# A decoder trunk on one core: the MLP's second product with two of its seven products on shared PSUM banks, and the LayerNorm ahead of the MLP on ScalarE

## The chip, the cores and the metric

The kernel runs on one core of a Trainium2 chip. TensorE (PE) multiplies into PSUM, VectorE (DVE), ScalarE (ACT) and GpSimd (POOL) work element by element, SyncE (SP) issues DMAs. Each engine runs its own instructions in their order and waits for others by semaphores. The metric is the time of one execution on the device in microseconds; the median of several runs is compared.

## The reference

Two layers of a post-norm decoder: a token mixer, then an MLP, with a LayerNorm behind each. The sequence has 1024 rows, the model 1024 columns, the MLP 4096. Cut to what the change touches:

```python
def layer_norm(x, g, b):
    mu = jnp.mean(x, axis=-1, keepdims=True)
    var = jnp.mean(jnp.square(x - mu), axis=-1, keepdims=True)
    return (x - mu) * lax.rsqrt(var + LN_EPS) * g + b

for l in range(DEPTH):
    ...
    h = layer_norm(DEEPNORM_ALPHA * h + mix, ln1_g[l], ln1_b[l])
    ff = jnp.square(jax.nn.relu(h @ w_up[l])) @ w_down[l]
    h = layer_norm(DEEPNORM_ALPHA * h + ff, ln2_g[l], ln2_b[l])
```

All is float32. The kernel splits each operand into a high and a low part and makes three matmuls (high·high, high·low, low·high) for one product.

## The kernel before

**Data.** The residual stream is `zs`, eight tiles `z` of 128 rows by 1024 columns. Eight PSUM banks of 128x512 come from four rings: `pg` has three (allocated by `p_g`), `ps` two, `pt` two, `po` one.

**The MLP by chunks.** `w_up`'s 4096 columns are done in eight chunks of 512 (`NCH`). For a chunk, `up_steps(c)` makes the hidden values of all rows and `down_steps(c)` multiplies them by the 512 rows of `w_down` and adds the outcome to `zs`. Both treat their matrices as 2x2 quarters and make seven products of quarters in place of eight (the scheme of Strassen and Winograd), whose results are added to the quarters of the output. The first chunk's up product is plain (`up_plain(0)`, in two halves of the rows, 96 matmuls to a half and a column block of 512) and the last chunk's down product is plain too (`last_down`), so a layer has seven calls of `down_steps`: one behind `up_plain`, and six that alternate with `up_steps`. `run` goes through the steps; for each it first prepares the next step's operands and then does the matmuls.

**A down product.** The seven steps stand at the end of `down_steps`, in the order first, second, p5, p6, p3, p7, p4. `prep` copies the left operand `a` to its high part on ACT (L1161, `sa`), subtracts on DVE for the low part, and splits the weights into `wdh` (ACT) and `wdl` (DVE). Where a step's operand is a sum (the tiles `s` and `u`, the weights `wd`), DVE forms it just ahead of that. A step makes four groups, one for each 128 of its 512 rows, 6 matmuls each, so 24 a step and 168 in all. `bank` tells where a group accumulates: "x" is a set of four banks (two `ps`, two `pt`) which p6, p7 and p4 add to after the first step; "f" is a fresh `pg` for each group. After each group, DVE adds the bank to the z quarters named in the step's tail, (th, d): rows 4·th to 4·th+3 of the tiles, half d of the columns (`add(zc, zc, ps)`, L971 in the profile). A bank can be filled anew, or added to, once that read is done.

**The LayerNorm ahead of the MLP.** Behind the output projection, for each pair of z tiles, `ln_unit` takes the statistics (`ln_stats`) and normalizes in place on DVE (L154). `to_act` transposes the tiles on PE by blocks of 128x128 into `pt`, applies gain and offset on ACT on the way out (`f`, L212), and splits the outcome into `mh` (ACT, L215) and `ml` (DVE, L216), the MLP's operands. Behind `up_plain(0)` in the code, `residual` multiplies each normalized z by the row `gb` and adds `bb` on DVE (L817, L818); `sums_of_input` forms sums of the `f` tiles for later chunks.

**What sets the order.** The instructions of each engine are put in order by a scheduler ahead of time, with its own estimate of when each can run and with priorities (`boost()` around weight splits). The order in the code only breaks ties, so the order on each engine can change far from an edit.

Of the kernel before, what the change touches and what calls it, by code (L numbers as in the profile page):

```python
# [9 lines left out]
F32 = mybir.dt.float32  # L10
# [5 lines left out]
ALU = mybir.AluOpType  # L16
# [28 lines left out]
def trunk_kernel(ctx, tc, x, ln_in_g, ln_in_b, w_in, conv_w, conv_b, rg_wa, rg_ba, rg_wx, rg_bx, rg_lambda,  # L45
# [26 lines left out]
    def t_z(shape, nm, dt=F32):  # L72
        return big.tile(shape, dt, tag="z", name=nm, bufs=NZ)

    def t_u(dt, shape, nm):
        return big.tile(shape, dt, tag="u", name=nm, bufs=4)
# [4 lines left out]
    def t_s(shape, nm):  # L81
        return sm.tile(shape, F32, tag="s", name=nm, bufs=10)

    def p_g():
        return pg.tile([P, 512], F32, tag="g", name="pg")
# [19 lines left out]

    K = {}
    K["eps"] = cpool.tile([P, 1], F32, name="eps")
    V.memset(K["eps"], LN_EPS)
    A.activation(t_s([P, 1], "warm"), K["eps"], AF.Sqrt)

# [17 lines left out]
            V.scalar_tensor_tensor(out=r, in0=t, scalar=1.5, in1=r, op0=ALU.add, op1=ALU.mult)  # L128
        return r

    def ln_stats(zs):

        n = len(zs)
        st, mv = t_s([P, n, 2, 6], "lnst"), t_s([P, n, 2], "lnmv")
        for i, z in enumerate(zs):
            for j in range(2):
                V.bn_stats(out=st[:, i, j, :], in_=z[:, 512 * j:512 * j + 512])  # L137
            V.bn_aggr(out=mv[:, i, :], in_=st[:, i].rearrange("p a b -> p (a b)"))

        var = mv[:, :, 1]  # L140
        ve, r, t = t_s([P, n], "lnve"), t_s([P, n], "lnr"), t_s([P, n], "lnt")
        A.activation(r, var, AF.Sqrt, bias=K["eps"])
        V.tensor_scalar(out=ve, in0=var, scalar1=LN_EPS, scalar2=-0.5, op0=ALU.add, op1=ALU.mult)
        V.reciprocal(out=r, in_=r)
        V.tensor_tensor(out=t, in0=r, in1=r, op=ALU.mult)  # L145
        V.tensor_tensor(out=t, in0=t, in1=ve, op=ALU.mult)  # L146
        V.scalar_tensor_tensor(out=r, in0=t, scalar=1.5, in1=r, op0=ALU.add, op1=ALU.mult)  # L147
        return mv[:, :, 0], r
# [728 lines left out]
    for l in range(DEPTH):  # L877
# [43 lines left out]
        gb, bb = residual_rows(ln1_g[l], ln1_b[l])  # L921
        act = Act("m")

        keep = [[t_u(F32, [P, 4, 512], f"f{h}{g}") for g in range(2)] for h in range(2)]
        for cqs in ((0, 1), (2,), (3,)):
            ws = [load_cols(w_out[l], [(cq * 256, 256)], "wo") for cq in cqs]
            for nt in range(NT):
                for i, cq in enumerate(cqs):
                    ps = p_g()[:, :256]
                    gemm_tm(ps, ws[i], ya, nt)  # L930
                    zc = zs[nt][:, cq * 256:cq * 256 + 256]
                    V.tensor_tensor(out=zc, in0=zc, in1=ps, op=ALU.add)
                if cqs[-1] == 3 and nt % 2:
                    ln_unit(zs[nt - 1:nt + 1])
                    to_act(act, zs[nt - 1:nt + 1], nt - 1, *[c[:, 8 * l:8 * l + 8] for c in ln1], keep)

        nxt = Act("x") if l + 1 < DEPTH else None
        NCH = DFF // 512
# [203 lines left out]
        def down_steps(c, base):  # L1142

            def t_v(nm):
                return t_wf(nm) if c == 0 else t_z([P, 2, 512], nm)

            b, op, s_ = {}, {}, []
            x = []

            def load(j, k):  # L1150
                t = t_raw(f"wd{j}{k}").rearrange("p (f d) -> p f d", f=2) if j == 0 else t_v(f"wd{j}{k}")
                r0 = c * 512 + 256 * j
                nc.sync.dma_start(out=t, in_=w_down[l][r0:r0 + 256, 512 * k:512 * k + 512].rearrange("(f p) d -> p f d", p=P))
                b[j, k] = t

            def prep(a, w):
                av = []
                for f in range(2):
                    hi, lo = [mid.tile([P, 512], F32R, tag="m", name=f"sa{p}", bufs=NM) for p in range(2)]
                    src = a.parts[f] if isinstance(a, Quarter) else a[:, f]  # L1160
                    A.activation(hi, src, AF.Copy)  # L1161
                    sub(lo, src, hi.bitcast(F32))
                    av.append((hi, lo))
                hi, lo = split_w(w.rearrange("p f d -> p (f d)"), "wd")
                op["a"], op["w"] = av, [v.rearrange("p (f d) -> p f d", f=2) for v in (hi, lo)]

            def step(pre, operands, bank, first, *sums):
                got = []

                def p_():  # L1170
                    pre()
                    prep(*operands())
                    got.append((op["a"], op["w"]))

                def r_():
                    a, w = got[0]
                    if not x:
                        x.extend((p_s(), p_s(), p_t(), p_t()))
                    for i in range(4):
                        t = slice(i * P, i * P + P)  # L1180
                        ps = x[i] if bank == "x" else p_g()
                        mm3_on(ps, [((a[f][0][:, t], a[f][1][:, t]), (w[0][:, f, :], w[1][:, f, :])) for f in range(2)], first)
                        for th, d in sums:
                            zc = zs[4 * th + i][:, 512 * d:512 * d + 512]
                            add(zc, zc, ps)
                return p_, r_

            def loads():
                for jk in ((0, 0), (1, 0), (0, 1), (1, 1)):
                    load(*jk)  # L1190

            def p5():
                s_.append(t_v("s1"))
                base[1][0].by(lambda u, v, s: add(s, u, v), base[1][1], s_[0])
                sub(b[0, 0], b[0, 1], b[0, 0])

            def p6():
                base[0][0].by(lambda u, s: sub(s, s, u), s_[0])
                sub(b[0, 0], b[1, 1], b[0, 0])

            def p3():
                base[0][1].by(lambda u, s: sub(u, u, s), s_[0])

            def p7():
                base[1][0].by(lambda u, v: sub(u, v, u), base[0][0])
                sub(b[0, 1], b[1, 1], b[0, 1])

            def p4():
                sub(b[1, 0], b[1, 0], b[0, 0])

            nop = lambda: None
            return [
                step(loads, lambda: (base[0][0], b[0, 0]), "x", True, (0, 0)),
                step(nop, lambda: (base[0][1], b[1, 0]), "f", True, (0, 0)),
                step(p5, lambda: (s_[0], b[0, 0]), "f", True, (1, 1), (0, 1)),
                step(p6, lambda: (s_[0], b[0, 0]), "x", False, (0, 1)),
                step(p3, lambda: (base[0][1], b[1, 1]), "f", True, (0, 1)),
                step(p7, lambda: (base[1][0], b[0, 1]), "x", False, (1, 1)),
                step(p4, lambda: (base[1][1], b[1, 0]), "x", False, (1, 0))]

# [35 lines left out]
                        nc.sync.dma_start(out=spill[nt - 1 + i], in_=zp[i])  # L1256

        base = up_plain(0)
        for z in zs:
            residual(z, gb, bb)  # L1260
        sums_of_input()
        moving = [None]
        fixed = [fetch(1, t_u), fetch(2, t_u)]
# [87 lines left out]
```

## Time and profile before

| | |
|---|---|
| median of 3 runs | 2537.6 us (2537.27 to 2538.57) |
| the profiled execution | 2534.94 us, span of its instructions 2533.2 us |
| PE busy | 2409.7 us (95%), 14692 matmuls |
| DVE busy | 1803.8 us (71%) |
| ACT busy | 1105.7 us (44%) |
| POOL busy | 122.1 us (5%) |

A timeline row gives the start of an instruction (or of several alike in a row, x2), its length, its engine, its line and its operands as output <- inputs; in brackets, how long its engine sat idle before it and what it waited for. Matmuls overlap: the length of one is its own time from entry to end, and the distance of two starts is what it costs in a row. The same holds for the other engines, where the next instruction may start before the last has drained. A window row gives the length of a stretch and each engine's busy time in it with the count of starts, then the clock that was granted to TensorE (1.00 is 2.4 GHz, .50 is 1.2 GHz).

### The profile page before, as it was taken

The numbers are of one execution on the slowest core, as the hardware profiler recorded it, in microseconds if no ns is written. First come the engines' busy times: TensorE is split into PE (matmuls) and PEld (weight loads), VectorE is DVE, ScalarE is ACT, GpSimd is POOL, SyncE is SP. The second block draws the span as 40 slices with busy tenths as digits, with TensorE's granted clock in tenths as the row PEclk, the third lists the DMA queues.
The fourth block names the chain that finished last, engine by engine and source line by source line (L and its number), as shares of the span: only waits on it lengthen the run. The fifth ranks groups of instructions, "written<-read, shape, count | busy, mean of one in ns | idle before, by whom it ended". The sixth has DMA issues, their size and how long they took to land. (4 is left out here: it accounts for less than half of the span.)

```text
span 2533.2 us, 36546 instructions
## 1 busy us (share of the span) xinstructions
PE 2409.7 (95%) x14692; PEld 2014.7 (80%) x14692; DVE 1803.8 (71%) x3105; ACT 1105.7 (44%) x1710; POOL 122.1 (5%) x190
## 2 busy tenths in 40 slices
PE   7999999999899999999999999999998999999997
PEld 6887888897678777877798877889976777777875
DVE  6578764747976787778745868456577867787768
ACT  6433556415444334433462346472353444344442
POOL 0002000000100000000000110000001000000003
PEclk9999999999999999999999989999999999999999
DMA  5215102211833223232221321121226333223222
GB/s 190 64 50 169 35 28 84 68 51 34 282 108 125 92 75 133 100 115 78 92 81 34 113 97 39 40 84 51 67 98 223 112 114 120 92 75 133 100 83 83
DMA packets 131073, 241.41 MB, mean 95 GB/s; under 512 B 8924, under 2 KB 89432, under 8 KB 122712
## 3 DMA queue, kind: packets, MB, share of 16 engines
q1 hardware_dynamic: 110128, 135.55, 16.6%
q0 software_dynamic: 19648, 102.80, 11.4%
q8 instruction: 116, 1.90, 0.3%
q10 hardware_dynamic: 1128, 0.72, 0.1%
q14 instruction: 53, 0.43, 0.1%
HBM read 201.29 MB, written 37.75 MB: 94 GB/s over the span
## 5 line engine op out<-in xcount | busy, mean ns | idle before, releaser
L261 PE MATMUL pg<-wdh,sa 128*128 128x512 f32 x672 | 233.9, 409 | 31.4 <-DVE z L971 24.7
L222 ACT ACTIVATE wuh<-wu 128x1024 fp32r<-128x1024 f32 x106 | 112.2, 1059 | 319.4 <-DVE wu L968 187.9
L223 DVE TENSOR_TENSOR wul<-wu,wuh 128x1024 fp32r<-128x1024 f32 x106 | 130.3, 1229 | 147.0 <-ACT wuh L222 67.9
L261 PEld LDWEIGHTS pg<-wdh,sa 128*128 128x128 f32 x672 | 128.7, 192 | 84.1 <-DVE z L971 31.3
L222 ACT ACTIVATE wdh<-wd 128x1024 fp32r<-128x1024 f32 x120 | 126.6, 1056 | 132.8 <-DVE wd L968 59.5
L223 DVE TENSOR_TENSOR wdl<-wd,wdh 128x1024 fp32r<-128x1024 f32 x120 | 147.5, 1229 | 44.9 <-PE pt L261 22.4
L261 PE MATMUL ps<-wdh,sa 128*128 128x512 f32 x448 | 149.4, 398 | 26.7 <-DVE z L971 21.0
L252 PE MATMUL pg<-woh,yh 128*128 128x256 f32 x512 | 147.7, 290 | 1.0 <-DVE bvg L637 1.0
L971 DVE TENSOR_TENSOR z<-z,pg 128x512 f32<-128x512 f32 x224 | 146.9, 696 | 0.0
L253 PE MATMUL pg<-wol,yh 128*128 128x256 f32 x512 | 146.3, 287 | 0.0
L261 PE MATMUL pt<-wdh,sa 128*128 128x512 f32 x448 | 145.8, 391 | 0.0
L254 PE MATMUL pg<-woh,yl 128*128 128x256 f32 x512 | 145.5, 287 | 0.0
L261 PE MATMUL pg<-s,wuh 128*128 128x512 f32 x448 | 137.7, 389 | 1.4 <-ACT wuh L222 1.4
L261 PE MATMUL pt<-s,wuh 128*128 128x512 f32 x448 | 137.9, 389 | 0.0
L261 PE MATMUL pg<-wdl,sa 128*128 128x512 f32 x336 | 132.3, 401 | 0.0
L261 PEld LDWEIGHTS ps<-wdh,sa 128*128 128x128 f32 x448 | 82.9, 188 | 54.6 <-issue 26.5
L968 DVE TENSOR_TENSOR sa<-u,sa 128x512 fp32r<-128x512 f32 x140 | 91.5, 698 | 29.5 <-ACT sa L1161 29.5
L261 PE MATMUL pg<-mh,wuh 128*128 128x512 f32 x280 | 109.2, 390 | 0.0
L261 PE MATMUL pg<-ml,wuh 128*128 128x512 f32 x280 | 109.1, 390 | 0.0
L261 PE MATMUL pg<-mh,wul 128*128 128x512 f32 x280 | 108.6, 389 | 0.0
L252 PEld LDWEIGHTS pg<-woh,yh 128*128 128x128 f32 x512 | 99.1, 194 | 1.9 <-PE pt L715 1.4
L253 PEld LDWEIGHTS pg<-wol,yh 128*128 128x128 f32 x512 | 99.3, 194 | 0.1
(388 smaller groups left out, 6833.0 us busy)
## 6 DMA issues: line engine op xcount, KB each, us to landing
s<-sd POOLq DMA_DIRECT2D x64, 1024.0 KB, 6.9
wu<-in_w_up_dram SPq DMA_DIRECT2D x64, 512.0 KB, 3.8
wd<-in_w_down_dram SPq DMA_DIRECT2D x64, 512.0 KB, 3.6
sd<-sx POOLq DMA_DIRECT2D x32, 512.0 KB, 3.8
spill<-z SPq DMA_DIRECT2D x16, 512.0 KB, 4.7
wb<-in_w_in_dram SPq DMA_DIRECT2D x16, 512.0 KB, 6.3
rs<-spill POOLq DMA_DIRECT2D x32, 256.0 KB, 4.2
resid<-rs POOLq DMA_DIRECT2D x32, 256.0 KB, 3.6
```

The lines of the kernel that those rows point to most:

```text
L222: A.activation(hi, raw, AF.Copy)
L223: V.tensor_tensor(out=lo, in0=raw, in1=hi.bitcast(F32), op=ALU.subtract)
L252: T.matmul(ps, ah, bh, start=(i == 0), stop=False)
L253: T.matmul(ps, ah, bl, start=False, stop=False)
L254: T.matmul(ps, al, bh, start=False, stop=(i == n - 1))
L261: T.matmul(ps, a, b, start=(first and i == 0 and j == 0), stop=(i == n - 1 and j == 2), skip_group_check=not first)
L968: V.tensor_tensor(out=out, in0=x, in1=y, op=ALU.subtract)
L971: V.tensor_tensor(out=out, in0=x, in1=y, op=ALU.add)
```

## The change

There are two parts. In `down_steps` the fifth product gets four banks of its own, "y": three `pg` and the `po`. They are added to z's quarter (1,1) only and then kept; p3 goes on accumulating on them (no `start`), and its adds to (0,1) bring both products. So the fifth product's four adds to (0,1) are gone.

In the LayerNorm ahead of the MLP the statistics are kept in constant tiles `mv` and `rs`. ACT writes the normalized rows to new tiles `zu` (scale r, offset −mean·r, formed by a small DVE instruction), which the transposes read; z itself stays as it was. The residual becomes (z − mean)·gb, then times r plus bb, as two DVE instructions a tile, which need z and the statistics and no longer wait for the transposes.

```diff
     K["eps"] = cpool.tile([P, 1], F32, name="eps")
+    K["mv"], K["rs"] = cpool.tile([P, NT, 2], F32, name="mv"), cpool.tile([P, NT], F32, name="rs")
...
-    def ln_stats(zs):
+    def ln_stats(zs, mv=None, r=None):
...
+        mv, rs = K["mv"], K["rs"]
...
                 if cqs[-1] == 3 and nt % 2:
-                    ln_unit(zs[nt - 1:nt + 1])
-                    to_act(act, zs[nt - 1:nt + 1], nt - 1, *[c[:, 8 * l:8 * l + 8] for c in ln1], keep)
+                    pair = slice(nt - 1, nt + 1)
+                    mean, r = ln_stats(zs[pair], mv[:, pair, :], rs[:, pair])
+                    nb = t_s([P, 2], "lnnb")
+                    V.scalar_tensor_tensor(out=nb, in0=mean, scalar=-1.0, in1=r, op0=ALU.mult, op1=ALU.mult)
+                    zu = [t_z([P, DM], "zu") for _ in range(2)]
+                    for i in range(2):
+                        A.activation(zu[i], zs[nt - 1 + i], AF.Identity, scale=r[:, i:i + 1], bias=nb[:, i:i + 1])
+                    to_act(act, zu, nt - 1, *[c[:, 8 * l:8 * l + 8] for c in ln1], keep)
...
-            x = []
+            x, y = [], []
...
                         t = slice(i * P, i * P + P)
-                        ps = x[i] if bank == "x" else p_g()
+                        if bank == "y" and first:
+                            y.append(p_g() if i < 3 else p_o())
+                        ps = x[i] if bank == "x" else y[i] if bank == "y" else p_g()
...
-                step(p5, lambda: (s_[0], b[0, 0]), "f", True, (1, 1), (0, 1)),
+                step(p5, lambda: (s_[0], b[0, 0]), "y", True, (1, 1)),
                 step(p6, lambda: (s_[0], b[0, 0]), "x", False, (0, 1)),
-                step(p3, lambda: (base[0][1], b[1, 1]), "f", True, (0, 1)),
+                step(p3, lambda: (base[0][1], b[1, 1]), "y", False, (0, 1)),
...
         base = up_plain(0)
-        for z in zs:
-            residual(z, gb, bb)
+        for i, z in enumerate(zs):
+            V.scalar_tensor_tensor(out=z, in0=z, scalar=mv[:, i, 0:1], in1=gb, op0=ALU.subtract, op1=ALU.mult)
+            V.scalar_tensor_tensor(out=z, in0=z, scalar=rs[:, i:i + 1], in1=bb, op0=ALU.mult, op1=ALU.add)
```

The order of the engines' instructions moves with it. First DVE in a steady down product, from the adds of the second product on (a number behind a name tells tiles apart, and differs between the two kernels). Before:

```order
L971 TENSOR_TENSOR z<-z,pg 128x512
L968 TENSOR_TENSOR sa_10140<-s_10132,sa_10139 128x512
L971 TENSOR_TENSOR z<-z,pg 128x512
L968 TENSOR_TENSOR wd_10040<-wd_10046,wd_10040 128x1024
L971 TENSOR_TENSOR z<-z,pg 128x512
L968 TENSOR_TENSOR s_10132<-s_10132,u_9864 128x1024
L971 TENSOR_TENSOR z<-z,pg 128x512
L968 TENSOR_TENSOR wd_10042<-wd_10042,wd_10040 128x1024
L971 TENSOR_TENSOR z<-z,pg 128x512 x2
L223 TENSOR_TENSOR wdl<-wd_10040,wdh 128x1024
L968 TENSOR_TENSOR u_9933<-u_9933,s_10132 128x1024
L971 TENSOR_TENSOR z<-z,pg 128x512 x2
```

After:

```order
L981 TENSOR_TENSOR z<-z,pg 128x512
L978 TENSOR_TENSOR sa_9546<-s_9538,sa_9545 128x512
L981 TENSOR_TENSOR z<-z,pg 128x512
L978 TENSOR_TENSOR wd_9446<-wd_9452,wd_9446 128x1024
L981 TENSOR_TENSOR z<-z,pg 128x512
L978 TENSOR_TENSOR s_9538<-s_9538,u_9270 128x1024
L981 TENSOR_TENSOR z<-z,pg 128x512
L981 TENSOR_TENSOR z<-z,po 128x512
L978 TENSOR_TENSOR wd_9448<-wd_9448,wd_9446 128x1024
L981 TENSOR_TENSOR z<-z,pg 128x512
L226 TENSOR_TENSOR wdl<-wd_9446,wdh 128x1024
L978 TENSOR_TENSOR u_9339<-u_9339,s_9538 128x1024
```

Before, pairs of adds of `pg` follow the second product's four single ones, one ahead of `wdl` and the next behind it; now a `po` add and single `pg` adds stand there.

Next PE in the same place, from the end of the fifth product into the sixth (`ps`, `pt`) and the first matmul of the third. Before:

```order
L261 MATMUL ps<-wdh,sa_9617 128x512 x2
L261 MATMUL pt<-wdh,sa_9617 128x512 x2
L261 MATMUL pg<-wdh,sa_9571 128x512
L261 MATMUL pg<-wdl,sa_9571 128x512
L261 MATMUL pg<-wdh,sa_9572 128x512
L261 MATMUL pg<-wdh,sa_9575 128x512
L261 MATMUL pg<-wdl,sa_9575 128x512
L261 MATMUL pg<-wdh,sa_9576 128x512
L261 MATMUL ps<-wdl,sa_9617 128x512 x2
L261 MATMUL pt<-wdl,sa_9617 128x512 x2
L261 MATMUL pg<-wdh,sa_9666 128x512
```

After:

```order
L264 MATMUL pg<-wdh,sa_9546 128x512
L264 MATMUL ps<-wdh,sa_9587 128x512 x2
L264 MATMUL pt<-wdh,sa_9587 128x512 x2
L264 MATMUL ps<-wdl,sa_9587 128x512 x2
L264 MATMUL pt<-wdl,sa_9587 128x512 x2
L264 MATMUL pg<-wdh,sa_9632 128x512 x2
L264 MATMUL po<-wdh,sa_9632 128x512
```

Before, the fifth product's last six matmuls stand between the sixth's first four and next four; now they are ahead of the sixth product, and the third's first matmuls go to `pg` twice and `po` once, at the place where one `pg` matmul stood.

Last, ACT in layer 0 around the end of `up_plain`'s first half, whose last group is read by the u of line 991 (1001 in the changed file). Before:

```order
L212 ACTIVATE f_5230<-pt,lnc_848 128x256
L215 ACTIVATE mh_6200<-f_5230 128x2x256
L212 ACTIVATE f_5230<-pt,lnc_848 128x256
L215 ACTIVATE mh_6200<-f_5230 128x2x256
L991 ACTIVATE u_6351<-pg 128x512
L212 ACTIVATE f_5231<-pt,lnc_848 128x256
L992 ACTIVATE u_6351<-u_6351 128x512
L212 ACTIVATE f_5231<-pt,lnc_848 128x256 x2
L215 ACTIVATE mh_6220<-f_5231 128x2x256
```

After:

```order
L1001 ACTIVATE u_6361<-pg 128x512
L215 ACTIVATE f_5233<-pt,lnc_850 128x256
L944 ACTIVATE zu<-z,lnnb,rs 128x1024
L215 ACTIVATE f_5233<-pt,lnc_850 128x256
L1002 ACTIVATE u_6361<-u_6361 128x512
L218 ACTIVATE mh_6228<-f_5233 128x2x256
L215 ACTIVATE f_5232<-pt,lnc_850 128x256
L218 ACTIVATE mh_6228<-f_5233 128x2x256
L215 ACTIVATE f_5232<-pt,lnc_850 128x256 x2
L218 ACTIVATE mh_6208<-f_5232 128x2x256
```

The last group of the first half is u_6351 before and u_6361 after; the second half's first operand is mh_6200 before and mh_6208 after. Before, the last two parts of that operand stand ahead of u_6351; now they are behind u_6361 (the first of them is the last row here), with a zu of 128x1024 in between.

## Rows read from the trace of the kernel before

**Rows 1.** The page, part 1: busy time, share of the span, instructions
```profile
PE 2409.7 (95%) x14692; PEld 2014.7 (80%) x14692; DVE 1803.8 (71%) x3105; ACT 1105.7 (44%) x1710; POOL 122.1 (5%) x190
```

**Rows 2.** PE's waits over the span: engine, line, releaser: sum, times, longest (us)
```profile
PE pg L261 <- DVE z L971: 24.7, 27, 3.7
PE ps L261 <- DVE z L971: 21.0, 12, 1.8
PE po L506 <- DVE df L497: 8.8, 5, 4.1
```

**Rows 3.** Timeline of PE, a steady chunk: start, us, operation, [idle before <- releaser]
```profile
984.65 0.84 PE L261 MATMUL pg<-wdh,sa 128*128 128x512 f32 x3
...
989.04 0.50 PE L261 MATMUL pg<-wdh,sa 128*128 128x512 f32 x1 [0.16 <-DVE z L971]
...
999.60 0.47 PE L261 MATMUL pg<-wdh,sa 128*128 128x512 f32 x1 [0.99 <-DVE z L971]
1000.11 0.73 PE L261 MATMUL ps<-wdh,sa 128*128 128x512 f32 x2
...
1009.68 0.47 PE L261 MATMUL ps<-wdh,sa 128*128 128x512 f32 x1 [1.79 <-DVE z L971]
...
1016.58 0.39 PE L261 MATMUL pg<-mh,wuh 128*128 128x512 f32 x1
...
1018.85 0.39 PE L261 MATMUL pg<-ml,wuh 128*128 128x512 f32 x1
...
1080.49 0.47 PE L261 MATMUL pg<-wdh,sa 128*128 128x512 f32 x1 [1.01 <-DVE z L971]
```

**Rows 4.** Windows, down product and up product: start:end, length, busy time of each engine
```profile
979.00:1027.00 48.00, 44.95 (x192) 35.35 (x191) 46.22 (x61) 17.33 (x23) 0.00 (x0) 1.00 0.19 63
1027.00:1060.00 33.00, 33.00 (x147) 27.35 (x146) 15.92 (x19) 16.77 (x21) 2.11 (x4) 1.00 0.48 168
```

**Rows 5.** Timeline of DVE in the same chunk
```profile
995.89 1.23 DVE L223 TENSOR_TENSOR wdl<-wd,wdh 128x1024 fp32r<-128x1024 f32 x1
997.03 1.23 DVE L968 TENSOR_TENSOR u<-u,s 128x1024 f32<-128x1024 f32 x1
...
1008.83 1.30 DVE L971 TENSOR_TENSOR z<-z,ps 128x512 f32<-128x512 f32 x2
1010.03 1.30 DVE L971 TENSOR_TENSOR z<-z,pt 128x512 f32<-128x512 f32 x2
```

**Rows 6.** Groups by line and shape, count | busy, mean ns; durations of two lines
```profile
L1161 ACT ACTIVATE sa<-u 128x512 fp32r<-128x512 f32 x140 | 79.8, 621 | 31.9 <-PE pt L261 25.2 <-DVE u L968 4.8 <-DVE sa L968 1.1
...
L212 ACT ACTIVATE f<-pt,lnc 128x256 f32<-128x256 f32 x64 | 34.2, 561 | 32.8 <-PE pt L207 32.4
...
L154 DVE TENSOR_SCALAR z<-z,lnmv,lnr 128x1024 f32<-128x1024 f32 x32 | 25.1, 824 | 0.3
...
L170 ACT ACTIVATE z<-z,lnnb,lnr x7: 1240/1245/1247, 2484.1 to 2521.6; 128x1024 f32<-128x1024 f32 x7
...
L165 DVE SCALAR_TENSOR_TENSOR z<-z,lnr,lnp x2: 747/750/752, 2528.5 to 2529.2; 128x512 f32<-128x512 f32 x2
```

**Rows 7.** Windows at layer 0's LayerNorm ahead of the MLP; then PE's timeline there
```profile
585.00:590.00 5.00, 3.58 (x14) 2.04 (x15) 5.00 (x7) 4.93 (x11) 0.00 (x0) 0.91 0.44 141
590.00:595.00 5.00, 4.05 (x14) 2.14 (x12) 5.00 (x9) 3.94 (x9) 0.00 (x0) 0.50 0.19 68
595.00:600.00 5.00, 4.93 (x14) 4.01 (x15) 5.00 (x9) 2.15 (x6) 0.00 (x0) 0.57 0.00 0
...
595.41 0.78 PE L253 MATMUL pg<-ml,wuh 128*128 128x512 f32 x1
```

**Rows 8.** Window of layer 0's first chunk, down product; then DVE's timeline there
```profile
627.00:690.00 63.00, 53.67 (x212) 40.97 (x211) 62.79 (x78) 29.86 (x41) 11.73 (x22) 0.92 0.81 271
...
627.82 2.36 DVE L817 TENSOR_TENSOR z<-z,lnp 128x1024 f32<-128x1024 f32 x2
...
631.82 2.35 DVE L818 TENSOR_TENSOR z<-z,lnp 128x1024 f32<-128x1024 f32 x2
```

More of the change, by code (lines that the diff above doesn't have):

```diff
@@ L129, in rsqrt_small @@
         return r
-    def ln_stats(zs):
+    def ln_stats(zs, mv=None, r=None):
         n = len(zs)
-        st, mv = t_s([P, n, 2, 6], "lnst"), t_s([P, n, 2], "lnmv")
+        st = t_s([P, n, 2, 6], "lnst")
+        mv = t_s([P, n, 2], "lnmv") if mv is None else mv
         for i, z in enumerate(zs):
@@ L140, in ln_stats @@
         var = mv[:, :, 1]
-        ve, r, t = t_s([P, n], "lnve"), t_s([P, n], "lnr"), t_s([P, n], "lnt")
+        ve, t = t_s([P, n], "lnve"), t_s([P, n], "lnt")
+        r = t_s([P, n], "lnr") if r is None else r
         A.activation(r, var, AF.Sqrt, bias=K["eps"])
```

## Prediction

> **What bounds the kernel now.** I began with the busy times of the engines: TensorE (PE) is busy for 2409.7 of the 2533.2 us span [rows 1]. So PE sets the time, and all that a change with the same matmuls can win lies in PE's idle time and in matmuls that run slower than they could. The table of PE's waits [rows 2] says where that is: the two largest entries, 24.7 and 21.0 us, are MLP matmuls (L261) that wait for VectorE (DVE) to add a finished product to z (L971), since only then is a PSUM bank free.
>
> Next, one steady chunk of the MLP on PE's timeline [rows 3]. A `pg` matmul waits .16 us at 989.04 and .99 at 999.60, a `ps` matmul 1.79 at 1009.68, and the same stop comes back at 1080.49: the period is 1080.49 − 999.60 = 80.89 us. Ten matmuls without a stop take 1018.85 − 1016.58 = 2.27 us, .227 each, and a chunk has 336 (7 × 24 in the down product, 7 × 24 in the up product), which is 76.3 us. A chunk loses 80.9 − 76.3 = **4.6 us**: 2.94 in these three stops and some 1.7 around them, in late restarts (the first two behind the stop at 999.60 start .51 apart, not .227). There are six such chunks in each layer, 12 in all.
>
> The windows [rows 4] say why: in the 48 us of the down product DVE is busy for 46.22, in the 33 us behind it, in the up product, for 15.92 while PE is busy without a gap. DVE is the bound of the down product and has nothing to do afterwards. What leaves DVE's row there comes off the time, until PE or the operands' preparation is next.
>
> **The down product: fifth product kept on banks of its own.** The matmuls stay, 168 in a down product. Out of DVE's row go four adds of 128x512 (the fifth product's second destination; the third's adds now bring both). Four such adds in a row on DVE's timeline are a pair at 1008.83 and a pair at 1010.03 [rows 5]: 1.20 us for two, .60 each, so 4 × .60 = 2.4 us a chunk.
>
> I walked PE's new order with these times, from PE's first `pg` matmul of the second product at 984.65 on [rows 3]. Second and fifth product are 48 matmuls, 48 × .227 = 10.9: PE reaches the sixth product at 995.5. Its first four (`wdh`) need what is there; the next four need `wdl`, split by DVE. Ahead of that split stand six adds in both orders (before: four of the second product and a pair of the fifth; now: four of the second, two of the fifth), so it ends as before, 995.89 + 1.23 = 997.12 [rows 5]. PE stops for 997.12 − 996.45 = .7. The four `wdl` matmuls take PE to 998.1. Then, in the middle of the sixth product, PE's order has the third's first matmuls, whose operand is u after DVE's subtraction (997.03 + 1.23 = 998.26) and ACT's copy (.62, mean of L1161 in [rows 6]): 998.9 to 999.0, a second stop of .9. From there 39 matmuls are left of the two products, 8.9 us, to 1007.9. DVE by then is 2.4 us earlier: it takes the sixth product's `ps` at 1006.4, not 1008.83, so the seventh product starts at about 1008 without a stop, where before it started at 1009.68, with six matmuls of the third product left behind it. At equal work PE is 1.6 + 6 × .227 = 3.0 us earlier.
>
> So the stops are .7 + .9 = 1.6 in place of 2.94, **a listed gain of 1.3 us** as the least, and 4.6 − 1.6 = **3.0 us** as the most, if all slow restarts go with the old stops. Two new stops restart as well, at about .25 each by the first matmuls behind the stop at 999.60 (.51 − .227 = .28): I take 4.6 − 1.6 − .5 = **2.5**, rounded down to 2.4 for a stop of .16 that may stay. In 12 chunks that is −29 us (−16 to −36).
>
> All eight PSUM banks are taken between fifth and third product: four x, three `pg`, one `po`. Nothing else asks for one there, because the up product's first group comes after the third in PE's order; the wait for free banks is replaced by a wait for operands, which is in the walk.
>
> **LayerNorm on ScalarE (ACT).** DVE loses 16 normalizations of .82 us and gets 8 small operations; the adds of the residual become as many scalar_tensor_tensor. Two of 128x512 at the kernel's end take .75 each [rows 6], where an add of that size has .60 from start to start and 1.30 for two: for 32 of 128x1024 some .1 more each, 3 us of DVE in all, of which only what falls into DVE's full stretch counts. ACT gets 16 instructions of 128x1024. The trace has seven such, with scale and bias per partition, at 1.245 [rows 6].
>
> The Trainium skill, *ScalarE: Activation LUTs*, "Rules for kernel authors", says to put multiply and add on VectorE, not on ScalarE, and gives a budget of about .3 us an instruction and .83 ns an element, by which a row of 1024 would be an estimated 1.15 us. The trace agrees in direction and nearly in size (1.245 against .82). By that rule alone this half of the change is a loss; it is the second rival below.
>
> Where do these 1.245 us lie? At 585 to 590 us ACT is busy for 4.93 of 5 us and at 590 to 595 for 3.94, and PE, in its transposes, only for 3.58 and 4.05, with the clock down at .50, the 1.2 GHz level [rows 7]. So ACT, which empties the transposes' banks, is the bound in those 10 us, with DVE. But the order moves too. Before, 30 transposes surround PE's first three up matmuls, now 18 do: the third pair's come after the first half's gemms have begun. So these start without pause some 3 us sooner than at 595.41 [rows 7], and the half ends as much sooner. Behind it, however, the 14 transposes in a row and the second half's operands wait for ACT, in whose row stand now, from the first half's last group (u_6361) to the second half's operands: u, its square and three `mh`, each 128x512 as L1161 (.62), five f (.56) and one zu (1.245), 3.1 + 2.8 + 1.2 = 7.1 us [rows 6]; before, the `mh` stand ahead of that u. So the second half starts 7.1 − 3 = 4.1 us late, and the clock falls again: from 595 to 600 it was .57 [rows 7], 5 × .43 = 2.2 us lost. The second half ends 6.3 us late.
>
> What hides it: chunk 0 of the down product behind it is DVE's. From 627 to 690 DVE is busy for 62.79 of 63 us [rows 8] and PE for 53.67, so PE has 9.3 us to spare. Two pairs of the residual lie inside this stretch (627.82 and 631.82, 2.36 + 2.35 = 4.7 us), because they waited for the last transposes; now they wait for the copies to zu and are done earlier. DVE's first residual pair there starts at 627.82, its second ends at 634.2; the last split of the LayerNorm that stands between them I put at 629.9 in the new order (f and mh of the last pair, 4 × .56 + 2 × .62, and the split, behind the operands above), with nothing of the residual behind it: some 3 us to the good, as 1.1 us of other work was done in between. Four adds less in chunk 0 (2.4) make 5.4. PE, 6.3 late, has 9.3 to lose it in. I set LayerNorm and chunk 0 together at **−1 us a layer**, −2 in all, between −5 a layer (DVE's 5.4 fully paid out) and +10 (6.3 not absorbed, and 3.7 for three more zu ahead of what is late).
>
> The rest of the difference, a shifted order in the second layer's mixers, has the same instructions; I cost it at nothing, within 2 us either way, as the nearest wait there, L506 for DVE, is 8.8 us in five, 1.8 each [rows 2].
>
> **Sum.** −29 − 2 = −31 us. Against the profiled execution, 2534.9 (span 2533.2 and 1.7 around it), that is 2504; the median of the runs is 2.7 above it, so 2537.6 − 31 = **2506.6**.
>
> **Rivals.**
> *Only the listed stops go.* The slow restarts stay whatever the stops' number: 1.3 × 12 = 16, LayerNorm at nothing: **2522**. For it: two new stops stand where three were. Against: the restarts are seen only behind stops.
>
> *The LayerNorm is bound by ScalarE and is not hidden.* If chunk 0's stops on PE are for operands, which come from what the late second half yields, they move along with it and nothing is absorbed: +10 a layer against −29: **2528**. For it: ACT's 4.93 of 5 us [rows 7]. Against: DVE's unbroken row from 627 to 690.
>
> *Slower: PE stands behind the third product's first matmuls.* They stay where they were, in the middle of the sixth product, and PE works in order. Before, they waited for a free bank (.99 at 999.60); now they need DVE's add from the very bank that they write to, and in DVE's row two of these four adds stand behind the subtraction, and the last behind a `wdl` too. All eight banks are held meanwhile, so nothing else can go on. If DVE is late, the stop, .9 in my walk, grows; by the length of the fifth product, on whose end these adds hang, that is 24 × .227 = 5.4 us. The gain of 31 us is gone from 31 / 12 = 2.6 us more a chunk than I walked, about half of this; at the full 5.4 it is 12 × 5.4 − 31 = +34, **2572**. Against it: before, DVE had six adds in place of two ahead of the third product's first adds, and the fifth product's fourth bank is now filled ahead of the others, so its add comes early. The Trainium skill, *PSUM — Partial Sum Buffer*, "Summary: rules for kernel authors", says to empty PSUM promptly; the fifth product now stays on its banks over the length of a second one. By that the time would be this rival's. No row of before shows eight held banks; the nearest is the wait of 1.79 for a `ps` bank [rows 3], below the 2.6 that decide.
>
> *No change.* The operands of the later products, not the evictions, prove to be what DVE delivers last, and the seventh product starts at 1009.7 as before; the adds saved are idle time of DVE. Then −2 at most: **2536**. Against: in DVE's row the eviction of `ps` at 1008.83 is behind all of these operands [rows 5].
>
> **How the numbers follow.** A measurement of this kernel tells about .2% (5 us) from no change. Chances: forecast .60 (2496 to 2514), listed stops only .17, LayerNorm not hidden .13, slower .04, no change .06. The first three are faster by more than 5 us: .90; same .06; slower .04. The range runs from −36 − 10 (2492) to 2524, which takes in the first two cases and the nearer part of the third.
>
> **What would show it.** The step of DVE's adds: 56 fewer adds of 128x512 from `pg`, with `po` now among them. The chunk: a period of 78.5 us, not 80.9, DVE below 44 us busy in the down product, no wait of a `ps` matmul for z, and two new waits, a `ps` matmul for `wdl` at .7 and a `pg` matmul for ACT's `sa` at .9. LayerNorm: PE idle and at the lower clock between the halves for 4 to 7 us, chunk 0's stops down by about as much. I am wrong if the period stays above 79.6, or if the stretch from the third pair's transposes to the end of chunk 0 is more than 5 us longer than before.

## The result and the profile after

The changed kernel takes 2493.8 us (median of 4 runs, 2492.1 to 2495.0) against 2537.4 before: 43.6 us less, a ratio of .9827 with a 95% interval of .981 to .9844. The profiled execution has a span of 2492.8 us, 40.4 less than before. The forecast was 2506.6 with a range from 2492 to 2524. The time lies inside the range, near its lower end, and 2 us below the band of 2496 to 2514 that had the largest chance. The way and the mechanism in the chunks hold; the gain came out at 43.6 us where 31 were forecast.

The page of the changed kernel, part 1 (before: [rows 1]):

```profile
PE 2394.6 (96%) x14692; PEld 2020.2 (81%) x14692; DVE 1761.2 (71%) x3041; ACT 1118.6 (45%) x1726; POOL 122.1 (5%) x190
```

The same matmuls, 15 us less of PE's busy time and 25 us less outside it. PE's waits, sums over the span (before: [rows 2]; line numbers are 3 to 13 higher in the changed file):

```profile
PE pg L264 <- ACT sa L1171: 8.8, 16, 0.6
...
PE ps L264 <- DVE wdl L226: 7.0, 12, 0.6
PE pg L264 <- DVE z L981: 6.2, 2, 3.1
...
PE ps L264 <- ACT sa L1171: 3.5, 2, 1.7
...
PE pt L210 <- ACT zu L944: 3.2, 4, 0.8
```

The 45.7 us of waits for the adds to z (24.7 and 21.0) are down to 6.2, in two stops, one in each layer's first down product. In their place stand twelve stops for the split `wdl` and sixteen for ACT's copy `sa`, .6 us at most each: waits for operands have taken the place of waits for banks.

A steady chunk on PE's timeline, from the first matmul of a down product to the first of the next (before: [rows 3]):

```profile
969.40 0.39 PE L264 MATMUL ps<-wdh,sa 128*128 128x512 f32 x1
...
986.17 0.61 PE L264 MATMUL pt<-wdh,sa 128*128 128x512 f32 x2
987.37 0.73 PE L264 MATMUL ps<-wdl,sa 128*128 128x512 f32 x2 [0.59 <-DVE wdl L226]
987.94 0.63 PE L264 MATMUL pt<-wdl,sa 128*128 128x512 f32 x2
989.17 0.74 PE L264 MATMUL pg<-wdh,sa 128*128 128x512 f32 x2 [0.60 <-ACT sa L1171]
989.75 0.40 PE L264 MATMUL po<-wdh,sa 128*128 128x512 f32 x1
...
998.41 0.39 PE L264 MATMUL ps<-wdh,sa 128*128 128x512 f32 x1
...
1047.37 0.39 PE L264 MATMUL ps<-wdh,sa 128*128 128x512 f32 x1
```

The period is 1047.37 − 969.40 = 77.97 us (77.93 or 77.97 in the other chunks), where it was 80.89. The row at 998.41 is the seventh product: no wait ahead of it. Busy times in a whole chunk, down product and up product, first before, then after:

```profile
979.20:1026.10 46.90, 43.85 (x187) 34.43 (x186) 45.16 (x60) 17.13 (x23) 0.00 (x0) 1.00 0.19 62
1026.10:1060.10 34.00, 34.00 (x151) 28.16 (x150) 16.87 (x19) 16.87 (x21) 2.11 (x4) 1.00 0.46 163
```

```profile
969.40:1016.00 46.60, 45.41 (x199) 36.96 (x198) 44.49 (x58) 17.59 (x24) 0.00 (x0) 1.00 0.19 62
1016.00:1047.40 31.40, 31.40 (x141) 25.99 (x140) 15.13 (x17) 16.20 (x20) 2.11 (x4) 1.00 0.51 179
```

DVE (the third pair of numbers) still works for 44.49 of 46.60 us in the down product: it is still nearly as full there as PE (I had expected less than 44), but 2.4 us less over the whole chunk (59.62 for 62.03). PE's busy time falls by 1.0 us a chunk (77.85 to 76.81) at a granted clock of 1.00 in all four rows, some 12.5 us in the twelve chunks: the clock has no part in it, and the matmul behind a stop counts as busy for longer (.47 and .50 in [rows 3], .39 without a stop).

Where the 40.4 us of the span went, read off PE's timeline at three marks in each layer (last matmul of the output projection, first of chunk 0's down product, first of the next down product):

| us | before, layer 0 / 1 | after, layer 0 / 1 | difference |
|---|---|---|---|
| output projection to chunk 0 | 62.1 / 60.2 | 65.3 / 65.3 | +3.2 / +5.1 |
| chunk 0 to the next down product | 91.1 / 94.9 | 84.9 / 85.5 | −6.2 / −9.4 |
| from there to the last, plain down product (six chunks) | 485.5 / 485.4 | 467.7 / 467.7 | −17.8 / −17.7 |
| all else | | | +2.4 |

Of the last row, 2.1 us lie ahead of the first mark, in layer 0.

### The profile page after: what moved, and what is told of

It reads as the page before. It is cut to its first block, busy times and chain, and to the rows that moved or that the text cites. A ratio compares the mean times of both kernels' runs of the same rounds, so it can differ in the third digit from the quotient of the medians.

```text
span 2492.8 us, 36411 instructions
## 1 busy us (share of the span) xinstructions
PE 2394.6 (96%) x14692; PEld 2020.2 (81%) x14692; DVE 1761.2 (71%) x3041; ACT 1118.6 (45%) x1726; POOL 122.1 (5%) x190
## 4 chain that ended last, share of the span: by engine, by line
PE 75%; DVE 15%; ACT 5%; DMA 3%; issue 2%; POOL 0%; DVEq 0%; SPq 0%; POOLq 0%; ACTq 0%
PE pg L264 16%; PE pg L255 11%; PE pg L256 11%; PE pg L257 11%; PE pt L264 10%; PE ps L264 5%; DVE z L981 3%; PE po L264 2%; DVE wdl L226 2%; PE po L608 2%; PE pt L600 2%; DVE wd L978 1%; DVE u L978 1%; PE pt L210 1%; DMA rs<-spill 1%
## 5 line engine op out<-in xcount | busy, mean ns | idle before, releaser
L264 PE MATMUL pg<-wdh,sa 128*128 128x512 f32 x560 | 184.1, 398 | 18.4 <-ACT sa L1171 8.8
L226 DVE TENSOR_TENSOR wdl<-wd,wdh 128x1024 fp32r<-128x1024 f32 x120 | 146.5, 1222 | 43.6 <-PE pt L264 21.9
L264 PEld LDWEIGHTS pg<-wdh,sa 128*128 128x128 f32 x560 | 105.0, 190 | 48.8 <-ACT sa L1171 15.7
L264 PE MATMUL pg<-wdl,sa 128*128 128x512 f32 x280 | 107.7, 393 | 0.0
L264 PEld LDWEIGHTS pt<-wdh,sa 128*128 128x128 f32 x448 | 84.1, 188 | 17.6
```

The costliest lines, as they stand in the source:

```text
L226: V.tensor_tensor(out=lo, in0=raw, in1=hi.bitcast(F32), op=ALU.subtract)
L264: T.matmul(ps, a, b, start=(first and i == 0 and j == 0), stop=(i == n - 1 and j == 2), skip_group_check=not first)
```

## The experiments

The times of before that stand beside these runs are 2538.3 to 2538.4 us (medians of 7 to 13 runs); the changed kernel's 2493.8 is that of the section above, with 2537.4 beside it. One table first; the marks are those above. "To chunk 0" and "chunk 0" are the first two rows of the table above, layer 0 / 1.

| kernel | us | to chunk 0 | chunk 0 | period |
|---|---|---|---|---|
| before | 2538.3 | 62.1 / 60.2 | 91.1 / 94.9 | 80.91 |
| changed | 2493.8 | 65.3 / 65.3 | 84.9 / 85.5 | 77.95 |
| e1 LayerNorm part alone | 2534.4 | 65.2 / 65.1 | 86.0 / 86.0 | 80.91 |
| e2 adds kept | 2528.3 | 65.3 / 64.9 | 88.2 / 88.3 | 79.6 to 80.7 |
| e3 old banks, fewer adds | 2494.7 | 64.9 / 65.1 | 85.2 / 85.1 | 77.91 |
| e4 four more adds left out | 2479.4 | 65.3 / 65.8 | 84.2 / 84.6 | 76.68 |
| e5 down product's part alone | 2504.3 | 61.3 / 61.8 | 90.7 / 96.5 | 77.93 |
| e6 rows in place on ACT | 2488.2 | 60.7 / 60.3 | 86.3 / 86.8 | 77.93 |
| e7 new tiles by DVE | 2500.2 | 71.9 / 68.8 | 80.9 / 86.0 | 77.93 |
| e8 a difference on GpSimd | 2509.5 | 65.5 / 65.5 | 85.3 / 89.1 | 78.7 |
| e9 that difference later | 2489.8 | 65.5 / 65.4 | 88.1 / 86.3 | 77.16 |
| e10 last pair in place | 2507.4 | 63.7 / 65.1 | 93.2 / 93.0 | 77.92 |
| e11 e6 and e9 | 2481.2 | 62.0 / 61.7 | 86.2 / 86.5 | 77.16 |
| e12 e10 and e9 | 2488.0 | 63.6 / 63.7 | 87.6 / 87.1 | 77.16 |

**What in the down product brings the gain: adds or banks?** Three kernels take them apart.

e2, the new banks with the old number of adds:

```diff
-                step(p5, lambda: (s_[0], b[0, 0]), "y", True, (1, 1)),
+                step(p5, lambda: (s_[0], b[0, 0]), "y", True, (1, 1), (0, 1)),
```

> The changed kernel with the fifth product on its own banks as in the change, but added to both quarters as before: the four adds of 128x512 a down product come back, and nothing else (the fifth product is then counted twice in one quarter). Theory, DVE's row of adds is the bound: 4 x .60 = 2.4 us a chunk come back and the new banks have to wait for two adds each, period 80.3 to 81.5, time 2525 to 2540 us. Rival, the gain is in the banks (no third-product group asks for a free bank any more): period stays near 77.9, time 2492 to 2500.

Measured: 2528.3 us, ratio .9958 (.9943 to .9973), period 79.6 to 80.7. The six chunks of a layer take 481.0 and 480.1 us, so of the 35.5 us that the change gains there 25.7 are gone. The time is in the theory's range; the period, 80.1 on average, is a little below it. PE's timeline of a chunk:

```profile
998.53 0.73 PE L264 MATMUL ps<-wdl,sa 128*128 128x512 f32 x2 [1.78 <-DVE wdl L226]
...
1000.33 0.50 PE L264 MATMUL pg<-wdh,sa 128*128 128x512 f32 x1 [0.60 <-ACT sa L1171]
```

The stop for `wdl` is 1.78, not .59: the two adds that came back ahead of this split, 2 × .60, are just the difference.

e3, the old banks with the new number of adds:

```diff
-                step(p5, lambda: (s_[0], b[0, 0]), "y", True, (1, 1)),
+                step(p5, lambda: (s_[0], b[0, 0]), "f", True, (1, 1)),
...
-                step(p3, lambda: (base[0][1], b[1, 1]), "y", False, (0, 1)),
+                step(p3, lambda: (base[0][1], b[1, 1]), "f", True, (0, 1)),
```

> The changed kernel with the banks of before (fifth and third product on fresh banks each) but with the changed kernel's number of adds: the fifth product is left out of the quarter (0,1). Theory, DVE's adds are the bound: period within .5 us of 77.9, time 2488 to 2500 us. Rival, banks: the third product waits for a free bank as before (.99 a chunk), period 79 or more, time 2507 or more.

Measured: 2494.7 us, ratio .9826 (.9808 to .9845), the changed kernel's own time, with the banks of before. PE's timeline:

```profile
978.84 0.50 PE L264 MATMUL pg<-wdh,sa 128*128 128x512 f32 x1 [0.15 <-DVE z L981]
...
988.71 0.73 PE L264 MATMUL ps<-wdh,sa 128*128 128x512 f32 x2 [0.34 <-DVE sa L978]
```

The wait of .99 for a free bank [rows 3] is gone without a new bank. So the wait for banks was a wait for DVE's row, and with the fewer adds the four kept banks neither cost nor bring anything (2493.8 with them, 2494.7 without). With as many adds as before they do bring something: e2's chunks are 4.4 and 5.3 us a layer shorter than those of e1, which has the old banks (485.4 in both layers). That is about a quarter of the gain; whether the banks bring it or the order that changes with them is not shown. In the change, what the banks do is to make the fewer adds possible.

e4, the remaining four adds of the fifth product away too:

```diff
-                step(p5, lambda: (s_[0], b[0, 0]), "y", True, (1, 1)),
+                step(p5, lambda: (s_[0], b[0, 0]), "y", True),
```

> The changed kernel without the fifth product's four remaining adds to (1,1), which are left out of the result. Two of these adds stand ahead of the split that makes the sixth product wait .59. Theory, DVE's order is still the bound: this split ends 1.2 us sooner and its stop goes, the stop for the copy of u (.60) shrinks to .3 or less, period 76.5 to 77.0, time 2476 to 2485 us. Rival, what is left is bound by ScalarE or the weights' arrival: period stays at 77.6 to 77.9, time 2488 to 2494.

Measured: 2479.4 us, ratio .9766 (.975 to .9783), period 76.68, one stop left in the chunk:

```profile
981.22 0.73 PE L264 MATMUL ps<-wdh,sa 128*128 128x512 f32 x2 [0.21 <-DVE sa L978]
```

A chunk's 336 matmuls at .227 are 76.3 us, so this is nearly all that a chunk has to give: the changed kernel's remaining loss is DVE's too.

**The two parts alone.** e1 is the kernel of before with the LayerNorm part, e5 the kernel of before with the down product's part.

> The LayerNorm part of the change alone, with the down product of before. Theory: the chunks gain nothing (period 80.9 us); of the 5.2 us that the traces show between the output projection and the second chunk of the two layers, the larger part belongs to the four adds fewer in chunk 0, so 2534 to 2540 us. Rival A, LayerNorm pays by itself: 2530 or less. Rival B, it costs and the down product hid it: 2543 or more.

> The down product's part alone, with the LayerNorm of before. Theory, the parts add up: 12 chunks of 3.0 us (35.6) and two chunk 0 of 2 to 3 us, without the 4 us that the LayerNorm part alone gave: 2495 to 2500 us. Rival, ScalarE's LayerNorm costs at the boundary and only the early residual pays: 2492 or less.

Measured: e1 2534.4 us, ratio .998 (.997 to .9989); e5 2504.3, ratio .9868 (.9852 to .9885). Alone, LayerNorm gives 3.9 and the down product 34.0; together they give 43.6, 5.7 more than the sum. The table shows 3.3 of this in the first two columns (−7.3 us for the change, −6.0 for e1, +2.0 for e5): with the LayerNorm of before, chunk 0 does not gain from its four adds fewer (90.7 / 96.5, before 91.1 / 94.9); with the new one it stands at 85 to 86 either way. The time and the period of e1 are those of its theory, but not its reason: it gave the larger part of the gain ahead of the second chunk to the four adds, and e1, without these, has 6.0 of the 7.3 us in its trace. (That trace is of an execution of 2528.5 us, 6 below e1's median.) The theory of e5 expected chunk 0 to gain 2 to 3 us a layer, and missed the time by 4 us.

**Which half of the LayerNorm part helps?** e6 lets ACT normalize in place and takes back the residual of before; e7 keeps tiles and residual of the change and lets DVE write the rows. With e5 (neither) and the changed kernel (both) this is a square.

```diff
 e6
-                    zu = [t_z([P, DM], "zu") for _ in range(2)]
+                    zu = zs[pair]
...
-            V.scalar_tensor_tensor(out=z, in0=z, scalar=mv[:, i, 0:1], in1=gb, op0=ALU.subtract, op1=ALU.mult)
-            V.scalar_tensor_tensor(out=z, in0=z, scalar=rs[:, i:i + 1], in1=bb, op0=ALU.mult, op1=ALU.add)
+            residual(z, gb, bb)
 e7
-                        A.activation(zu[i], zs[nt - 1 + i], AF.Identity, scale=r[:, i:i + 1], bias=nb[:, i:i + 1])
+                        V.tensor_scalar(out=zu[i], in0=zs[nt - 1 + i], scalar1=mean[:, i:i + 1], scalar2=r[:, i:i + 1],
+                                        op0=ALU.subtract, op1=ALU.mult)
```

> The changed kernel with the rows normalized by ScalarE, but in place, and with the residual of before (which then waits for the transposes). Theory: the gain of the LayerNorm part comes from the residual that no longer waits, so without it 3 to 5 us a layer are lost in DVE's full stretch and nothing is left of the gain: 2498 to 2506 us. Rival, the gain is that DVE is rid of 16 x .82 us: 2492 to 2496.

> The changed kernel with the residual from mean and deviation as in the change, but the normalized rows written to their new tiles by DVE (16 x .82 us), not by ScalarE (16 x 1.25). Theory: ScalarE is the bound between the halves of the first up product, where two of its copies lie in front of the second half's operands; without them the second half starts 1 to 3 us sooner and the time is 2488 to 2492 us. Rival, DVE is full from 585 to 595 us and pays as much as ScalarE saves: 2493 to 2500.

| us | rows by DVE | rows by ACT |
|---|---|---|
| in place, residual of before | 2504.3 (e5) | 2488.2 (e6) |
| new tiles, residual from mean and deviation | 2500.2 (e7) | 2493.8 (changed) |

Both theories fell: e6 came out below its rival's range too, e7 at the upper end of its rival's. The rows on ScalarE gain 16.1 us in place and 6.4 with the new tiles. The early residual gains 4.1 us with DVE's LayerNorm and costs 5.6 with ACT's. How much of the three smaller numbers is the edit, and how much the order that the scheduler finds around it, is not separated (see e12 below). The trace shows what goes with the 5.6. ACT's timeline of the changed kernel, the third pair's two copies and the last tile's, and then e6's third and fourth pair:

```profile
596.75 1.25 ACT L944 ACTIVATE zu<-z,lnnb,rs 128x1024 f32<-128x1024 f32 x1 [1.03 <-DVE lnnb L941]
598.86 1.25 ACT L944 ACTIVATE zu<-z,lnnb,rs 128x1024 f32<-128x1024 f32 x1 [0.86 <-PE pt L210]
...
618.46 1.24 ACT L944 ACTIVATE zu<-z,lnnb,rs 128x1024 f32<-128x1024 f32 x1
```

```profile
583.44 2.37 ACT L944 ACTIVATE z<-z,lnnb,rs 128x1024 f32<-128x1024 f32 x2
...
602.24 2.38 ACT L944 ACTIVATE z<-z,lnnb,rs 128x1024 f32<-128x1024 f32 x2
```

In place, the third pair is done at 585.8; in the change it starts 13 us later, and the eighth tile 15 us later. The first of them waits for DVE's `lnnb`, the end of the statistics. In DVE's timeline of the changed kernel eight residual instructions of the first two pairs, 1.2 us each, stand ahead of it between 572.2 and 594.3; in e6 this `lnnb` is at 583.22 and the first residual at 585.95, behind it. The last of the eight, the `lnnb`, and a residual of the last pair:

```profile
593.09 1.28 DVE L1273 SCALAR_TENSOR_TENSOR z<-z,rs,lnp 128x1024 f32<-128x1024 f32 x1
...
596.55 0.16 DVE L941 SCALAR_TENSOR_TENSOR lnnb<-mv,rs 128x2 f32<-128x2 f32 x1
...
619.73 1.28 DVE L1272 SCALAR_TENSOR_TENSOR z<-z,mv,lnp 128x1024 f32<-128x1024 f32 x1 [5.98 <-ACT zu L944]
```

A residual that is ready early is put early into DVE's order, ahead of the statistics that the transposes need. The second of the pair waits for PE's transposes (.86), which free its place in the ring that it shares with z. That these delays make up the 5.6 us is argued, not shown.

e10 asks whether the tiles alone are to blame: its last pair is in place (`zu = zs[pair] if nt == NT - 1 else ...`, and `residual` for the last two tiles).

> The changed kernel with the last of the four pairs normalized in place by ScalarE and its residual as before; the other three pairs as in the change. Theory: in the change the eighth new tile waits for a free place in the ring that it shares with z, and with it the second half of the first up product; without it the first down product starts some 61 us after the output projection, not 65.3, and the time is 2486 to 2490 us. Rival: the order of ScalarE's copies makes the second half late, not the tile: 65 us and 2492 or more.

Measured: 2507.4 us, ratio .9879 (.9865 to .9894): by its numbers the rival, but most of the 13.6 us that it is above the change lie elsewhere. The eighth row block is started at 607.5 and not at 618.5, yet chunk 0 starts only 1.6 and .2 us sooner, so the last tile was not the cause. And chunk 0 itself is 8 us longer; the last pair's residual now stands in DVE's row at 630 to 636. That would be the price of a late residual, but e6 has it as late and a chunk 0 of 86.3. What of chunk 0's time is the residual and what the order that the scheduler finds around it stays open: its time ranges from 81 to 96.5 us over these kernels with nearly the same instructions.

**The two stops that are left.** The seventh step's weight difference (1.13 us) stands in DVE's row ahead of the split that the sixth product waits for. e8 gives it to GpSimd, e9 makes it wait for that split by writing it over the tile which the split reads; e11 is e6 with e9's edit, e12 is e10 with it.

```diff
 e8
-                sub(b[1, 0], b[1, 0], b[0, 0])
+                nc.gpsimd.tensor_tensor(out=b[1, 0], in0=b[1, 0], in1=b[0, 0], op=ALU.subtract)
 e9
-                sub(b[1, 0], b[1, 0], b[0, 0])
+                sub(b[0, 0], b[1, 0], b[0, 0])
...
-                step(p4, lambda: (base[1][1], b[1, 0]), "x", False, (1, 0))]
+                step(p4, lambda: (base[1][1], b[0, 0]), "x", False, (1, 0))]
```

> The changed kernel with one weight difference a down product, the seventh step's (128x1024, 1.13 us of DVE's row, ahead of the split that the sixth product waits for), computed by GpSimd, where the nearest row has 2.4 us for such an operation. Theory: the split ends 1.1 us sooner, the stop of .59 goes and the one of .60 shrinks, period 76.7 to 77.2, time 2480 to 2486 us. Rival, GpSimd and DVE slow each other down while both run, or the seventh step's weights come late: 2494 or more.

Measured: 2509.5 us, ratio .9888 (.9873 to .9903), 16 slower than the change; the rival. GpSimd's and DVE's timelines of e8, and what it does to PE:

```profile
984.56 2.39 POOL L1221 TENSOR_TENSOR wd<-wd,wd 128x1024 f32<-128x1024 f32 x1 [16.33 <-issue]
```

```profile
984.84 3.19 DVE L978 TENSOR_TENSOR s<-s,u 128x1024 f32<-128x1024 f32 x1
```

```profile
988.69 0.50 PE L264 MATMUL pg<-wdh,sa 128*128 128x512 f32 x1 [1.35 <-DVE z L981]
```

DVE's operation beside it takes 3.19 us; the same form alone takes 1.22. It ends at 988.03, 1.08 behind GpSimd's end at 986.95: it did next to nothing while GpSimd ran. PE's waits for adds to z are back at 25.2 us in 16 stops.

> The changed kernel with the seventh step's weight difference written over the tile that the sixth product's split reads, so that DVE makes it behind that split and not ahead of it; DVE's work is the same. Theory, what is left in a chunk hangs on DVE's order, not on its sum: the stop of .59 goes, that of .60 shrinks, period 76.7 to 77.2, time 2479 to 2485 us. Rival, DVE's sum is still the bound: the 1.1 us come back as a stop ahead of the seventh product, period 77.8 or more, time 2492 or more.

Measured: 2489.8 us, ratio .9806 (.9791 to .982). The period is 77.16, as the theory had it, with one stop of .34 in the chunk:

```profile
990.98 0.73 PE L264 MATMUL pg<-wdh,sa 128*128 128x512 f32 x2 [0.34 <-ACT sa L1171]
```

That is .79 × 12 = 9.5 us, but the time fell by 4 only (5 by the ratios) and lies above the expected 2479 to 2485: chunk 0 is 3.2 and .8 us longer than in the change. The intervals of the two ratios overlap, so only the shorter period is clear.

> The kernel with all rows normalized in place by ScalarE and the residual of before (2488), with the seventh step's weight difference behind the sixth product's split. Theory: both gains add, 2474 to 2479 us. Rival, with a shorter chunk something else is late: 2482 or more.

> Three pairs normalized into new tiles, the last in place, and the seventh step's weight difference behind the sixth product's split. Theory: 2472 to 2478 us, at or below the version with all pairs in place, as six tiles of the residual are early. Rival: the new tiles of the third pair wait as well and the version with all pairs in place is faster by 2 us or more.

Measured: e11 2481.2 us, ratio .9772 (.9757 to .9786), 57 us below before and 12.6 below the change: the fastest kernel here with the whole computation. It is 2 us above the range of its theory. e12 2488.0, ratio .9802 (.9786 to .9819): the rival, all rows in place is the better one by 7 us.

e9's edit is now measured in three surroundings, and gives 4.0 us in the change, 7.0 in e6 and 19.4 in e10. e12 and e10 show how far the order alone goes. They differ by that edit, which takes .76 us off a period; but chunk 0 is 5.6 and 5.9 us shorter in e12 (87.6 / 87.1 for 93.2 / 93.0) and starts as in e10 in layer 0 and 1.4 us sooner in layer 1. So an edit outside the LayerNorm moves these stretches by some 12 us in all, and of the differences that are put down to the LayerNorm's parts only the 16.1 us of e6 over e5 is larger.

## Why the prediction was right, and where it was not

**The steady chunk** is the main term, and its walk came out nearly instruction by instruction. Shifted by the two kernels' offset (984.65 to 974.84, 9.81 us), the sixth product was expected at 985.7 and started at 985.72; the split `wdl` at the end of DVE's walk, 987.3, at 987.31; the seventh product at about 998.2, at 998.41, without a stop. Both new stops are where they were put.

The step that failed is the deduction behind it. I put the gain at 2.4 us a chunk and it is 2.96 (35.5 / 12). The stops of the walk, .7 and .9, were counted from start to start; the 2.94 of before were listed idle times. The two are not the same: a matmul ends .39 behind its start where the next would start .227 behind it, so idle time begins .16 late. The listed stops of after are .59 and .60; by starts they are 987.37 − 986.63 = .74 and 989.17 − 988.40 = .77, and the matmuls right behind them (.34 apart, where I had read .51 off the row at 1000.11) lose .12 and .13 more: 1.76 of the 1.80 by which this chunk exceeds 336 matmuls at .2267 (76.17; 24 matmuls from 969.40 to 974.84 take 5.44). I had 2.2 left: 1.6 for the stops (1.51 came), .5 for the matmuls behind them (.25 came) and .1 for a stop of .16 that did not stay. The loss of before was 80.89 − 76.17 = 4.72 and not 4.6. Of the two ends, 1.3 and 3.0, the upper was right: −35.5 us in 12 chunks, not −29. That error of 6.5 us is half of the distance to the measured time.

**LayerNorm and chunk 0** were put at −1 us a layer and came out at −3.0 and −4.3 (first two rows of the first table). The parts had the right sign in layer 0: the first half's matmuls ran sooner (the 96th 31.8 us behind the output projection, before 36.8: 5.0, not 3), the second half began late (its fourth matmul at 40.2, before 37.9: +2.3, not +4.1; in layer 1 it is +4.1, from 36.1), and the clock fell again between the halves, to .70 and .62:

```profile
620.00:625.00 5.00, 3.28 (x12) 2.00 (x12) 4.20 (x5) 4.97 (x11) 0.00 (x0) 0.70 0.00 0
625.00:630.00 5.00, 5.00 (x17) 3.90 (x16) 0.69 (x1) 0.73 (x2) 0.00 (x0) 0.62 0.00 0
```

Chunk 0 started +3.2 and +5.1 late, not +6.3, and lost that again. What I had wrong is why chunk 0 could take it: I gave 3 us to the early residual and 2.4 to the four adds. By e5 the adds alone bring nothing there, and by e6 the early residual is not needed for it (86.3 and 86.8 with the late one). What does shorten it stays open: e7, with the rows on DVE, has the shortest chunk 0 of all in layer 0 (80.9) behind the latest start (71.9), and e10 and e12 differ there by nearly 6 us with the same LayerNorm. That the sign came out right is in part luck.

**The sum.** The chunks' 6.5 us and the LayerNorm's 5.3 (7.3 for 2), less the 2.4 of all else, take the forecast −31 to the −40.4 between the two traces. The last 3.2 us to −43.6 are the distance of the profiled executions from their medians (2.5 below before's, .8 above the changed kernel's).

**ScalarE against VectorE.** ACT's copy was priced at 1.245 us and took 1.24 (median of 16, against .82 on DVE), the residual's instructions at some .1 above an add and took 1.27 and 1.28 for 1.22 (the row gives shortest, median and longest in ns):

```profile
L944 ACT ACTIVATE zu<-z,lnnb,rs x16: 1228/1240/1247, 570.5 to 1843.9; 128x1024 f32<-128x1024 f32 x16
```

The rule of the Trainium skill that spoke against it (*ScalarE: Activation LUTs*, "Rules for kernel authors") holds for the single instruction and not for this kernel. In chunk 0 before, DVE is busy for 62.79 of 63 us and ACT for 29.86 [rows 8], and the kernels with the rows on the slower engine are 6.4 and 16.1 us faster than those with the rows on DVE.

**The rivals.** *Only the listed stops go* (2522): no, most of the slow restarts went with the stops. *The LayerNorm is not hidden* (2528): the late start was there, and chunk 0 took it in. *Slower, behind the third product's first matmuls*: that stop exists in every chunk, and is .60; to be decisive it had to be 2.6 longer. The profile puts it down to the operand, but DVE was hardly sooner: its last add ahead of these matmuls ends at 988.36 + .69 = 989.05, ACT's first copy at 988.49 + .62 = 989.11, and they start at 989.17.

```profile
988.36 0.69 DVE L981 TENSOR_TENSOR z<-z,pg 128x512 f32<-128x512 f32 x1
```

```profile
988.49 2.71 ACT L1171 ACTIVATE sa<-u 128x512 fp32r<-128x512 f32 x5 [1.45 <-DVE u L978]
```

By e3 the eight taken banks cost nothing, so the Trainium skill's rule to empty PSUM promptly (*PSUM — Partial Sum Buffer*, "Summary: rules for kernel authors") bound nothing here. *No change*: no.

## What to carry to other kernels

When an engine is full in one stage and idle in the next, count its row in that stage and ask which of its instructions the waiting engine's next operand stands behind: four adds of .60 us fewer here gave 2.96 us a chunk, and moving one operation behind a split gave .8 more without any less work (of 9.5 us in the chunks, 4 reached the total). A wait for a bank can be a wait for the engine that empties it: fewer adds on the old banks gave the whole gain, more banks with the old adds a quarter of it in the chunks. Where a scheduler orders the instructions, an edit can move other stages by several us, so read an edit's worth from its own stage and test it in more than one surrounding (one edit gave 4, 7 and 19 us here). A result that is made ready earlier may be scheduled ahead of what is needed first, as the early residual was ahead of the statistics.

## What had not been expected of the hardware

A GpSimd operation of 2.39 us held up a VectorE operation with two float32 operands in SBUF until its own end: 3.19 us in place of 1.22. It is so for all 14 of e8: 13 times such an operation of 128x1024 takes 3.1 to 3.3 us, once one of 128x512 takes 1.67 for .69, while two adds with one operand in a PSUM bank, which stand ahead of the latter beside GpSimd, keep their .68. The Trainium skill, *SBUF — State Buffer*, "Who interferes with whom", states that the two engines share a pair of ports under an exclusive lock; the row of e8 agrees.
